# Two recurrent heads in one group of small matmuls, pairs of column sums, and an edited order, in a hybrid decoder layer

## The chip, the cores and the metric

The kernel runs on one core of a Trainium2 chip. The metric is the device time of one execution in microseconds (us); a result is the median of several executions. TensorE (PE in the profile) multiplies matrices, VectorE (DVE) and ScalarE (ACT) work elementwise, GpSimd (POOL) does some fills and scalings and issues DMAs, SyncE (SP) issues DMAs. Matrix results land in PSUM, everything else lies in SBUF. PEld is TensorE's loading of the stationary operand, which the profile shows as an engine of its own.

## What is computed

One decoder layer for 512 positions of width 1024, in float32. The normed input goes through one projection into three head groups, and their outputs through one output projection; a gated feed-forward layer follows. Cut to the parts that the change touches:

```python
h = rmsnorm(x, norm_mix)
proj = h @ w_in
y_mla = mla_group(...)      # 4 heads, low-rank q and kv, per-head norm of q and k, causal softmax
y_hg = hgrn2_group(...)     # 4 heads of a gated recurrence, width 128
y_mem = mem_group(...)      # 4 heads, normed q and k, 256 fixed memory tokens
x = x + concat(rmsnorm(y_mla), y_hg, rmsnorm(y_mem)) @ w_out
h2 = rmsnorm(x, norm_ffn)
x = x + (silu(h2 @ w_gate) * (h2 @ w_up)) @ w_down

# the recurrence of one head, by position:  f = lb + (1 - lb) * sigmoid(f_raw);  k = 1 - f
# state = f[:, None] * state + k[:, None] * v[None, :];  o = q @ state
# then a norm of o over the head's 128 columns, and a SiLU gate
```

## The kernel before

The 512 positions are columns (S = 512, four blocks of 128, NB = 4), features are partitions (P = 128). Every large product is three matmuls of split operands: a float32 is split into a high part in the faster format (`split`, line 485: a copy or scaled copy on ScalarE) and a low part (a subtraction on DVE), and `mm3` (line 515) multiplies high by high, high by low and low by high. `piece` (line 500) does that for 512 columns of a weight that `load` (line 493) has brought into a `wr` buffer through SyncE's queue; hence the tiles `wh` and `wl`.

**The order of the work** is not that of the code. `Recorder` (line 46) records every operation with its operands and a priority: the class (0, 1 or 2, set by `rec.first`) times a million, plus the number of the operation. `run` (line 241) then plays the list through with a cost for each operation (`price`, line 184) and latencies between the engines, and picks for every engine, whenever it comes free, the ready operation of lowest priority; some operations it may give to another engine. Buffers belong to tags (`BUFS`, line 426: so many of each), and an operation that opens a new buffer waits until one of its tag is free. `issue` (line 362) writes out what comes out of it, so that each engine's instructions stand in that order; they run in it, one after the other, each waiting for its operands. All instructions carry line 382 or, for groups of small matmuls, line 379: the tile names tell them apart.

**Start (lines 465 to 618).** Eight gains come first, through ScalarE's queue (line 466). Seven warm-up matmuls of 128 columns run on TensorE (line 476). The input x comes in eight tiles `tm` through SyncE's queue; each is split into `xh` and `xl`, with the gain as scale. The weights of two first projections (`EARLY`, line 396) come in five pieces into `p` and `tc` buffers, two through ScalarE's queue and three through SyncE's between the x tiles. The squares of x are summed into `td`; `colsum` (line 534), `rms` and `spread` make the row of inverse norms `RX`, by which every projection is scaled.

**Groups of small matmuls.** An operation called `tiles` is a list of matmuls on 32 columns of the stationary operand, each at its own place of the array's columns; the planner prices it at 180 ns and 64 for each part that falls on one place. One part is two instructions in the trace. `colsum` sums over the partitions of a square: 16 parts for four blocks, with `ones` as the moving operand, on a `tr` or `mm` bank. It is called for RX, for each head's norm in the recurrence, for the memory tokens, for the two low-rank norms, for each of the four query heads of the latent attention (line 928) and of the memory attention (line 1123), and for group norms.

**The recurrence (lines 744 to 820).** For one head, `hg_levels` computes the 512 x 512 matrix of decayed scores in levels m = 1, 2, 4, ... 128: between two neighbouring runs of m positions the scores are products of q and k, scaled by decays towards the border between them. Up to level 16 this is `scores`: a group of 16 parts, 32 x 32 blocks on the diagonal; of its result DVE keeps by a mask (`copy_predicated` into `cc`) what belongs to the level, and the group for the diagonal itself comes first of all. Level 32 is a group of 8 parts, level 64 four matmuls, level 128 two. After each level q, k and the decays `tot` are multiplied up in place by three DVE operations; so a group must have read them before, and the next group needs the result. Scores lie in `p` (two buffers: one for the scores, one for the decays), `at` banks hold the results of the groups. `hg_out` splits the scores, multiplies them with the values, and norms. Lines 847 to 851 go through the heads one after the other, the projections of heads 2 and 3 between them. `hg_final` (line 822) applies the gate much later and splits the output into `xh` and `xl`, which the projections of x hold until then.

**Around it.** The memory tokens are loaded into `td` (line 859) and split into `mx`; `lowrank` (line 876) projects for the latent attention and puts its squares into `td`, which has three buffers. The norm over the latent attention's heads (`group_norm`, line 1040, called in line 1131) splits into `mx`. The output projection starts with the recurrent heads (`OUT_ORDER`), then the latent heads; the memory heads are added in a second pass. The feed-forward layer takes the second half of the time.

Of the kernel before, what the change touches and what calls it, by code (L numbers as in the profile page):

```python
# [45 lines left out]
class Recorder:  # L46
# [137 lines left out]
    def price(self, o, outs, ins):  # L184
# [55 lines left out]

    def run(self):
        ops = self.ops
        for o in ops:
# [151 lines left out]
WARM = 7  # L395
EARLY = {0: (1, "p", "scalar"), 1: (2, "p", "scalar"), 3: (2, "tc", "sync"), 5: (2, "tc", "sync"), 7: (1, "tc", "sync")}
# [10 lines left out]
def body(ctx, tc, t):  # L407
# [14 lines left out]
    def nm(p):  # L422
# [5 lines left out]
        "pth": 2, "ptl": 2, "qr": 1, "p": 2, "mx": 8, "cc": 2, "sm": 12, "sd": 8, "mm": 3, "at": 3, "tr": 2,  # L428
# [27 lines left out]


# [7 lines left out]
    with rec.first(0):  # L465
        A.dma_start(out=sm[:, 0:8], in_=t["sm"][:, 0:8])
# [67 lines left out]
    def colsum(sq, nblk):  # L534

        o = ps_ts()
        T.tiles(o[:, 0:2 * nblk], lhsT=sq, rhs=ones, parts=[
            (o[g:g + 32, 2 * b:2 * b + 2], sq[:, b * P + g:b * P + g + 32], ones, b == 0, b == nblk - 1)
            for b in range(nblk) for g in range(0, P, 32)
        ])  # L540
        return o[:, 0:2 * nblk].rearrange("p (b two) -> p b two", two=2)[:, :, 0]
# [26 lines left out]
    def heads(ap):  # L568
        return ap.rearrange("p (h d) -> p h d", d=P)


    with rec.first(0):
# [3 lines left out]
        early = ([], [])  # L576
        for k in range(KD):
            if k in EARLY:
                n, tag, q = EARLY[k]
                w = sb(tag)[:, :2 * n * P]  # L580
                getattr(rec, q).dma_start(out=w, in_=t["we"][:, 2 * k * P:2 * (k + n) * P])
                pc = piece(w, 0, 2 * n * P)
# [6 lines left out]
            split(r, hi, lo, smc("g_mix", k))  # L589
# [154 lines left out]
    def hg_levels(q, k_, tot):  # L744
        A_ = sb("p", (P, NB, P))
        tt = sb("p")
        C = sb("cc", (P, NB, 32))
        toff = 0

        def scores():  # L750

            o = ps_at()[:, 0:NB * 32].rearrange("p (b t) -> p b t", t=32)
            T.tiles(o, lhsT=k_, rhs=q, parts=[
                (o[g:g + 32, b], k_[:, b * P + g:b * P + g + 32], q[:, b * P + g:b * P + g + 32], b == 0, b == NB - 1)
                for b in range(NB) for g in range(0, P, 32)
            ])
            return o

        o = scores()
        V.tensor_tensor(C, o, eye.unsqueeze(1).broadcast_to([P, NB, 32]), ALU.mult)  # L760
        G.memset(A_, 0.0)
        V.tensor_tensor(q, q, tot, ALU.mult)
        m = 1
        while m <= 128:
            if m <= 16:
                o = scores()
                V.copy_predicated(C, lmask[:, LEVELS.index(m), :].unsqueeze(1).broadcast_to([P, NB, 32]), o)
                if m == 16:
                    for g in range(0, P, 32):
                        A.copy(A_[g:g + 32, :, g:g + 32], C[g:g + 32])  # L770
            elif m == 32:
                o = heads(ps_at())[:, :, :32]
                T.tiles(o, lhsT=k_, rhs=q, parts=[
                    (o[i:i + 32, b], k_[:, b * P + i:b * P + i + 32], q[:, b * P + i + 32:b * P + i + 64], b == 0, b == NB - 1)
                    for b in range(NB) for i in (0, 64)
                ])
                for i in (0, 64):
                    A.copy(A_[i:i + 32, :, i + 32:i + 64], o[i:i + 32])
            elif m == 64:
                o = heads(ps_at())[:64, :, :64]  # L780
                for b in range(NB):
                    T.matmul(o[:, b], lhsT=k_[:, b * P:b * P + 64], rhs=q[:, b * P + 64:(b + 1) * P], start=b == 0, stop=b == NB - 1, skip_group_check=True)
                A.copy(A_[:64, :, 64:], o)
            else:
                pts = [new_pt(2), new_pt(4)]
                for g, pt in enumerate(pts):
                    for x in pt:
                        G.memset(f(x)[:, 4 * g + 2, :], 0.0)
                o = ps_at()
                for i, s in enumerate((0, 2)):  # L790
                    T.matmul(o[:, i * P:(i + 1) * P], lhsT=k_[:, s * P:(s + 1) * P], rhs=q[:, (s + 1) * P:(s + 2) * P], start=i == 0, stop=i == 1, skip_group_check=True)
                for i in range(2):
                    split(o[:, i * P:(i + 1) * P], pts[i][0][:, 4 * i + 1, :], pts[i][1][:, 4 * i + 1, :])
            n = S // (2 * m)
# [662 lines left out]
```

## Time and profile before

| | |
|---|---|
| median of 3 runs | 729.4 us (727.81 to 729.68) |
| the profiled execution | 726.6 us |
| its span, first to last instruction | 724.7 us |
| mean granted TensorE clock | 0.995 |
| DMA traffic | 98.07 MB, 135 GB/s |
| LDWEIGHTS and matmuls on 32 columns in the recurrence | 832 each, 34.6 to 133.5 us |

A line of operations gives engine, operation, output<-inputs by tag (buffer numbers left out) and shape, then the count, busy time and mean duration, and the idle time of the engine ahead of them with what ended it. In the timeline the first two columns are start and duration in us, and square brackets hold the idle time ahead and its releaser. Matmuls are pipelined: one starts before the one ahead has ended, so their busy times overlap, and starts tell more than durations.

### The profile page before, as it was taken

What the parts mean: (1) busy time and instruction counts of PE and PEld (TensorE: products, weight loads), DVE (VectorE), ACT (ScalarE), POOL (GpSimd) and SP (SyncE); (2) the same over time, 40 slices, a digit from 0 to 9 for tenths busy, and PEclk for the clock granted to TensorE, in tenths of its full rate; (3) what the DMA queues carried; (4) which work ended last, traced back from release to release, by engine and by line L of the source; (5) the groups of instructions that cost most, each with busy time, mean ns of one, the idle gap of its engine ahead of it and who ended that gap; (6) DMA issues with size and microseconds to landing.
All of it is one profiled execution on the core that took longest, in us unless ns stands there. A gap on an engine that the chain in (4) does not pass through costs nothing.

```text
span 724.7 us, 13261 instructions
## 1 busy us (share of the span) xinstructions
PE 704.3 (97%) x4808; PEld 584.5 (81%) x4808; DVE 563.0 (78%) x1326; ACT 382.6 (53%) x726; POOL 93.0 (13%) x129
## 2 busy tenths in 40 slices
PE   7999999799999999899999999999999999999997
PEld 6888777678788887688686888888888899999886
DVE  6888889869988799897899979947548677538742
ACT  6743443437684487556477674635543355543420
POOL 0000000000000000000223323213202303410000
PEclk9999999999999999999999999999999999999999
DMA  8232122014621142121999999968958757942241
GB/s 277 76 107 70 60 89 74 24 38 140 195 97 34 55 137 92 49 59 44 263 266 214 256 215 226 229 151 220 219 146 165 180 135 172 219 110 41 66 131 72
DMA packets 47873, 98.07 MB, mean 135 GB/s; under 512 B 5568, under 2 KB 15680, under 8 KB 47808
## 3 DMA queue, kind: packets, MB, share of 16 engines
q1 hardware_dynamic: 33552, 73.75, 31.3%
q0 software_dynamic: 13824, 23.07, 20.3%
q8 instruction: 38, 0.62, 0.3%
q10 hardware_dynamic: 432, 0.40, 0.2%
q14 instruction: 27, 0.22, 0.1%
HBM read 95.11 MB, written 2.10 MB: 134 GB/s over the span
## 4 chain that ended last, share of the span: by engine, by line
PE 90%; DVE 6%; ACT 2%; issue 1%; DMA 0%; DVEq 0%; ACTq 0%
PE mm L382 47%; PE tr L382 21%; PE at L382 20%; PE at L379 1%; DVE wl L382 1%; PE tr L379 1%; DVE ptl L382 1%; DVE hd L382 1%; ACT L382 1%; DVE y L382 1%; DVE sm L382 0%; ACT p L382 0%; DMA tm<-in_xT 0%; DVE tm L382 0%; DVE tc L382 0%
## 5 line engine op out<-in xcount | busy, mean ns | idle before, releaser
L382 ACT CAST wh<-wr 128x512 fp32r<-128x512 f32 (+2 forms) x136 | 80.8, 598 | 113.7 <-PE mm L382 64.9
L382 DVE TENSOR_TENSOR wl<-wr,wh 128x512 fp32r<-128x512 f32 (+2 forms) x148 | 96.5, 657 | 33.2 <-issue 11.4
L382 PE MATMUL mm<-xh,wh 128*128 128x512 f32 x248 | 99.4, 406 | 5.5 <-ACT wh L382 3.2
L382 PE MATMUL mm<-xh,wl 128*128 128x512 f32 x248 | 100.2, 405 | 0.0
L382 PE MATMUL mm<-xl,wh 128*128 128x512 f32 x248 | 99.9, 404 | 0.2 <-DVE xl L382 0.2
L382 DVE TENSOR_TENSOR wl<-y,wh 128x512 fp32r<-128x512 f32 (+1 forms) x84 | 53.1, 637 | 42.2 <-PE tr L382 17.3
L382 ACT CAST wh<-y 128x512 fp32r<-128x512 f32 (+1 forms) x83 | 48.2, 582 | 66.5 <-PE at L382 34.2
L382 DVE TENSOR_TENSOR wl<-mx,wh 128x512 fp32r<-128x512 f32 (+1 forms) x72 | 45.6, 642 | 27.6 <-PE tr L382 14.8
L382 PE MATMUL mm<-wh,hd 128*128 128x512 f32 (+2 forms) x188 | 64.0, 366 | 0.7 <-ACT wh L382 0.7
L382 ACT CAST wh<-mx 128x512 fp32r<-128x512 f32 (+1 forms) x65 | 37.8, 584 | 40.9 <-PE at L382 22.1
L382 PEld LDWEIGHTS mm<-xh,wh 128*128 128x128 f32 x248 | 47.1, 191 | 14.5 <-ACT wh L382 3.6
L382 PEld LDWEIGHTS mm<-xl,wh 128*128 128x128 f32 x248 | 47.5, 191 | 8.7 <-DVE xl L382 0.7
L382 PEld LDWEIGHTS mm<-xh,wl 128*128 128x128 f32 x248 | 47.2, 190 | 8.4
L382 PE MATMUL at<-wh,hd 128*128 128x512 f32 (+1 forms) x132 | 49.7, 377 | 0.0
L382 POOL DMA_DIRECT2D y<-in_wu x36 | 32.5, 943 | 96.9 <-DVE wl L382 80.7
L382 PE MATMUL tr<-xl,wh 128*128 128x512 f32 x112 | 43.8, 391 | 0.0
L382 PE MATMUL tr<-xh,wl 128*128 128x512 f32 x112 | 43.7, 390 | 0.0
L382 PE MATMUL tr<-xh,wh 128*128 128x512 f32 x112 | 43.7, 390 | 0.0
L382 PEld LDWEIGHTS mm<-wh,hd 128*128 128x128 f32 x188 | 34.6, 188 | 5.8 <-ACT wh L382 1.1
L382 PE MATMUL mm<-wl,hd 128*128 128x512 f32 (+2 forms) x100 | 37.0, 370 | 0.2 <-DVE wl L382 0.2
L382 POOL MEMSET p<- 128x128 f32 (+1 forms) x12 | 3.7, 312 | 258.1 <-PE tr L382 116.8
L382 PE MATMUL mm<-wh,v 128*128 128x512 f32 (+1 forms) x96 | 36.1, 376 | 0.6 <-ACT v L382 0.6
(371 smaller groups left out, 1750.5 us busy)
## 6 DMA issues: line engine op xcount, KB each, us to landing
wr<-in_wf SPq DMA_DIRECT2D x19, 512.0 KB, 3.4
wr<-in_wd SPq DMA_DIRECT2D x16, 512.0 KB, 5.2
mx<-in_wg SPq DMA_DIRECT2D x24, 256.0 KB, 5.6
mx<-in_wu SPq DMA_DIRECT2D x24, 256.0 KB, 4.8
y<-in_wu POOLq DMA_DIRECT2D x24, 256.0 KB, 6.0
tm<-in_xT SPq DMA_DIRECT2D x16, 256.0 KB, 3.6
wr<-in_wt SPq DMA_DIRECT2D x8, 512.0 KB, 4.1
wr<-in_wo SPq DMA_DIRECT2D x8, 512.0 KB, 3.5
```

The costliest lines, as they stand in the source:

```text
L379: r = self.nc.tensor.matmul(get(a), lhsT=get(b), rhs=get(c), start=first, stop=last, skip_group_check=True)
L382: r = getattr(getattr(self.nc, o.eng), o.name)(*[get(a) for a in o.args], **{k: get(a) for k, a in o.kw.items()})
```

## The change

In words. (1) `hg_levels` takes two heads: scores, masks and buffers of both stand side by side in one group and one DVE call, and the diagonal shares the group of level 1 by writing q times its decay to a new `y` buffer. Level 64 becomes a group too. The decays are multiplied up in place, and both `p` buffers hold scores. Level 128 moves to `hg_out`. (2) `colsums` sums several squares in one group; the query heads of both attentions use it in twos. (3) All five pieces of first weights go through ScalarE's queue, the eight gains lie in the first of them, `hpi` is made on ScalarE by a multiplication instead of a fill on DVE, and the warm-up is twelve matmuls of 512 columns. (4) Memory tokens are loaded into `y` instead of `td`, the gated recurrent outputs go to `mx` instead of `xh` and `xl`, the latent attention's to `xh` and `xl` instead of `mx`. (5) The planner prices a group at 310 ns and 1.81 for each column streamed at one place (at least 35 for a part). (6) `NUDGE` adds a number to the priorities of 17 stretches of operations.

```diff
-                return 180 + 64 * len(o.kw["parts"]) / len({self._rng(p[0])[2] for p in o.kw["parts"]})
+                return 310 + 1.81 * sum(max(35, self._free(p[2])) for p in o.kw["parts"]) / len({self._rng(p[0])[2] for p in o.kw["parts"]})
...
+    NUDGE = ((2868, 2885, -117), (1571, 1576, -1459), (2382, 2422, -477), (1732, 1734, 30), (826, 835, 186), (957, 1012, 3), (5620, 5660, 284), (3804, 3864, -113), (987, 1017, 110), (2666, 2693, -105), (2466, 2475, -61), (2533, 2540, 37), (2401, 2403, -37), (3367, 3411, -5), (3019, 3021, 346), (16, 18, 380), (2, 19, 3),)
...
+        for a, b, d in self.NUDGE:
+            for o in ops[a:b]:
+                o.prio += d
...
-WARM = 7
-EARLY = {0: (1, "p", "scalar"), 1: (2, "p", "scalar"), 3: (2, "tc", "sync"), 5: (2, "tc", "sync"), 7: (1, "tc", "sync")}
+WARM = 12
+EARLY = {0: (1, "p"), 1: (2, "p"), 3: (2, "tc"), 5: (2, "tc"), 7: (1, "tc")}
...
-    with rec.first(0):
-        A.dma_start(out=sm[:, 0:8], in_=t["sm"][:, 0:8])
...
-            T.matmul(o[:, 0:P], lhsT=ones_r, rhs=ones_r, start=True, stop=True)
+            T.matmul(heads(o), lhsT=ones_r, rhs=ones_r.unsqueeze(1).broadcast_to([P, NB, P]), start=True, stop=True)
     hpi = cp.tile([P, 1], F32, name="hpi")
-    V.memset(hpi, float(np.pi / 2))
...
+    def colsums(sqs, nblk=NB):
+        o = ps_ts()[:, 0:2 * nblk * len(sqs)]
+        ks = [(i, b) for i in range(len(sqs)) for b in range(nblk)]
+        v = o.rearrange("p (i b two) -> p i b two", two=2, b=nblk)
+        T.tiles(o, ones, *sqs, parts=[
+            (v[g:g + 32, i, b], sqs[i][:, b * P + g:b * P + g + 32], ones, (i, b) == ks[0], (i, b) == ks[-1])
+            for i, b in ks for g in range(0, P, 32)
         ])
-        return o[:, 0:2 * nblk].rearrange("p (b two) -> p b two", two=2)[:, :, 0]
+        return v[..., 0]
...
+        for k, (n, tag) in EARLY.items():
+            w = ws[k] = sb(tag)[:, :2 * n * P + 8 * (k == 0)]
+            A.dma_start(out=w, in_=t["we"][:, 2 * k * P + 8 * (k > 0):2 * (k + n) * P + 8])
+        gain = ws[0][:, 2 * P:]
+
+        A.mul(hpi, ones[:, 0:1], float(np.pi / 2))
...
+    def hg_levels(hs):
+
+        N2 = range(len(hs))
+        As = [sb("p", (P, NB, P)) for i in N2]
+        C = sb("cc", (P, len(hs), NB, 32))
+        old, hs = hs, [(sb("y"), k_, tot) for q, k_, tot in hs]
+
+        def scores(sets):
+
+            n = len(sets) * len(hs)
+            o = ps_at()[:, 0:n * NB * 32].rearrange("p (n b t) -> p n b t", t=32, b=NB)
+            ps_ = [(b, g) for b in range(NB) for g in range(0, P, 32)]
+            all_ = [(i * len(hs) + j, h) for j in N2 for i, s in enumerate(sets) for h in (s[j],)]
+            T.tiles(o, *[x for i, h in all_ for x in h[:2]], parts=[
+                (o[g:g + 32, i, b], h[1][:, b * P + g:b * P + g + 32], h[0][:, b * P + g:b * P + g + 32], (i, b) == (all_[0][0], 0), (i, b) == (all_[-1][0], NB - 1))
+                for i, h in all_ for b, g in ps_
             ])
+            return [o[:, i * len(hs):(i + 1) * len(hs)] for i in range(len(sets))]
...
+        for (q, _, tot), (q1, _, _) in zip(old, hs):
+            V.tensor_tensor(q1, q, tot, ALU.mult)
...
+            if m == 1:
+                o, o1 = scores([old, hs])
+                V.tensor_tensor(C, o, eye.unsqueeze(1).unsqueeze(1).broadcast_to([P, len(hs), NB, 32]), ALU.mult)
+                put(o1, 1)
+            elif m <= 16:
+                put(scores([hs])[0], m)
...
+            hs = [(q, k_, step_up(q, k_, tot, m)) for q, k_, tot in hs]
...
-        hi = sb("xh", dt=F32R)
-        lo = sb("xl", dt=F32R)
+        hi = sb("mx", dt=F32R)
+        lo = sb("mx", dt=F32R)
         split(y, hi, lo)
         mix[4 + h] = (hi, lo)
...
-    for h in (0, 1):
-        yh.append(hg_out(h, *hg_levels(*qkf[h])))
-    qkf += [hg_in(2), hg_in(3)]
-    for h in (2, 3):
-        yh.append(hg_out(h, *hg_levels(*qkf[h])))
+    for h, st in enumerate(hg_levels(qkf)):
+        yh.append(hg_out(h, *st))
+    qkf = [hg_in(2), hg_in(3)]
+    for h, st in enumerate(hg_levels(qkf)):
+        yh.append(hg_out(2 + h, *st))
...
-            r = sb("td", (P, 2, NM))
+            r = sb("y", (P, 2, NM))
...
-            sq = sumsq([o])
-            V.tensor_copy(vq[:, :, h], colsum(sq, NB))
+            sq.append(sumsq([o]))
+            if h % 2:
+                V.tensor_copy(vq[:, :, h - 1:h + 1].rearrange("p b h -> p h b"), colsums(sq[-2:]))
...
-    group_norm(ym, 0, "g_mla", ("mx", "mx"))
+    group_norm(ym, 0, "g_mla", ("xh", "xl"))
```

More of the change, by code (lines that the diff above doesn't have):

```diff
@@ L455, in small, with heads @@
         return sb("sm" if rec.cls == 1 else "sd", (P, 16))[:, :n]
+    def heads(ap):
+        return ap.rearrange("p (h d) -> p h d", d=P)
     cst = cp.tile([P, 2 * P + 64], F32, name="cst")
@@ L534, in colsum @@
     def colsum(sq, nblk):
[L536 to L539, printed above, removed]
+        return colsums([sq], nblk)[:, 0]
+    def colsums(sqs, nblk=NB):
[5 more added lines that the diff above has]
+            for i, b in ks for g in range(0, P, 32)
         ])
-        return o[:, 0:2 * nblk].rearrange("p (b two) -> p b two", two=2)[:, :, 0]
+        return v[..., 0]
     def spread(r):
@@ L588, in body @@
             lo = sb("xl", dt=F32R)
-            split(r, hi, lo, smc("g_mix", k))
+            split(r, hi, lo, gain[:, k:k + 1])
             xg.append((hi, lo))
@@ L768, in hg_levels @@
                 if m == 16:
-                    for g in range(0, P, 32):
-                        A.copy(A_[g:g + 32, :, g:g + 32], C[g:g + 32])
+                    for j in N2:
+                        for g in range(0, P, 32):
+                            A.copy(As[j][g:g + 32, :, g:g + 32], C[g:g + 32, j])
             elif m == 32:
[L772 to L775, printed above, removed]
-                ])
@@ L777, in hg_levels @@
[L777 to L783, printed above, removed]
-            else:
[L785 to L793, printed above, removed]
@@ new lines, in hg_out @@
+    def hg_out(h, A_, q, k_, tot):
+        pts = [new_pt(2), new_pt(4)]
+        for g, pt in enumerate(pts):
+            for x in pt:
+                G.memset(f(x)[:, 4 * g + 2, :], 0.0)
+        o = ps_at()
+        for i, s in enumerate((0, 2)):
+            T.matmul(o[:, i * P:(i + 1) * P], lhsT=k_[:, s * P:(s + 1) * P], rhs=q[:, (s + 1) * P:(s + 2) * P], start=i == 0, stop=i == 1, skip_group_check=True)
+        for i in range(2):
+            split(o[:, i * P:(i + 1) * P], pts[i][0][:, 4 * i + 1, :], pts[i][1][:, 4 * i + 1, :])
+        step_up(q, k_, tot, 128)
```

83 lines of the change are left out of this document (41 added, 42 removed).

## The prediction

> **What bounds the kernel now.** I read the page first, then the windows by stage, then the timeline around single operations.
>
> ```profile
> span 724.7 us, 13261 instructions
> ...
> PE 704.3 (97%) x4808; PEld 584.5 (81%) x4808; DVE 563.0 (78%) x1326; ACT 382.6 (53%) x726; POOL 93.0 (13%) x129
> ...
> PE 90%; DVE 6%; ACT 2%; issue 1%; DMA 0%; DVEq 0%; ACTq 0%
> ```
>
> TensorE is busy for 704.3 of 724.7 us and carries 90% of the chain that ends last. So an edit is worth what it takes off TensorE's queue, plus what it takes out of the 20.4 us in which TensorE is idle. The windows say where that idle time lies (columns: window, its length, then busy us of PE, PEld, DVE, ACT, POOL; granted clock; DMA).
>
> ```profile
> 72.50:90.60 18.10, 18.10 (x196) 14.10 (x195) 15.87 (x43) 7.81 (x15) 0.91 (x3) 1.00 0.20 60
> ...
> 126.80:145.00 18.20, 14.26 (x174) 11.05 (x173) 15.49 (x49) 8.63 (x20) 0.20 (x1) 0.91 0.08 23
> ...
> 290.00:308.00 18.00, 14.44 (x95) 11.09 (x94) 15.20 (x40) 9.20 (x20) 0.96 (x2) 0.91 0.13 47
> ...
> 453.00:600.00 147.00, 146.84 (x692) 123.04 (x691) 97.82 (x158) 72.78 (x127) 34.60 (x40) 1.00 0.78 179
> ```
>
> The feed-forward half (the last row is 147 us of it) leaves nothing idle: what the change moves there can only lose. Two stages leave much: 3.94 us where the last recurrent head overlaps the memory loads (stall one), 3.56 us around the attention norm (stall two). In both the granted clock falls to 0.91. If it is halved for x us, the mean over 18 us falls by 9% when x is 3.3, and that costs up to 1.6 us more of TensorE time. So the stalls are worth up to 5.5 and 5.2 us.
>
> **The groups of small pieces.** What is one group worth? Two column sums stand close together, one of 32 instructions, one of 16; below them stands a score group, with 32 columns instead of two.
>
> ```profile
> 147.04 0.39 PE L382 MATMUL mm<-xh,wh 128*128 128x512 f32 x1
> 147.36 0.43 PE L379 MATMUL tr<-ones,tc 128*32 128x2 f32 x32
> 147.72 0.50 PE L382 MATMUL mm<-xl,wh 128*128 128x512 f32 x1
> 148.06 0.40 PE L382 MATMUL mm<-xh,wl 128*128 128x512 f32 x1
> 148.39 0.31 PE L379 MATMUL tr<-ones,td 128*32 128x2 f32 x16
> 148.62 0.50 PE L382 MATMUL mm<-xh,wh 128*128 128x512 f32 x1
> 148.96 0.39 PE L382 MATMUL mm<-xl,wh 128*128 128x512 f32 x1
> ```
>
> ```profile
> 70.28 0.39 PE L382 MATMUL mm<-xl,wh 128*128 128x512 f32 x1
> 70.50 0.40 PE L382 MATMUL mm<-xh,wl 128*128 128x512 f32 x1
> 70.83 0.46 PE L379 MATMUL at<-tm,tm 128*32 128x32 f32 x32
> 71.22 0.50 PE L382 MATMUL mm<-xh,wh 128*128 128x512 f32 x1
> 71.56 0.39 PE L382 MATMUL mm<-xl,wh 128*128 128x512 f32 x1
> ```
>
> Busy times overlap here, so I count from start to start. With no group between them, one matmul starts 0.22 us after the other (70.28 to 70.50); I use 0.23. From 147.04 to 148.06 lie two such steps and the group of 32: 1.02 - 0.46 = 0.56 us. From 148.06 to 148.96 lie two steps and the group of 16: 0.90 - 0.46 = 0.44. Sixteen instructions more cost 0.12, so 32 cost 0.24, and the rest, 0.32, is paid once for a group whatever is in it. The score group: 70.50 to 71.56 is 1.06 - 0.46 = 0.60; less 0.24, 0.36 is paid once.
>
> ```profile
> L379 PE MATMUL at<-tm,tm x832: 189/196/247, 34.6 to 133.5; 128*32 128x32 f32 x167
> ```
>
> 832 instructions are 24 groups of 32 and 4 of 16 (level 32). For a pair of heads the code goes from 12 groups of 32 to one of 128 and four of 64: 7 fixed parts fewer. Level 32 goes from two groups to one, and level 64, written as single matmuls until now, from two sets to one; I price that set at the same 0.36 by its likeness, an estimate between nothing and twice that. Nine times 0.36 is 3.24 a pair, 6.5 us for both. The number of instructions is the same. The four query heads of the latent attention and of the memory attention now share a column sum in twos: 4 groups fewer, 4 x 0.32 = 1.3. Together **7.8 us**, all on TensorE's queue; bounds 5.2 (two thirds, if a large group hides its drain less well) and 9.
>
> [...]
>
> What hides the rest of this edit is DVE, which has slack (78%): it writes each first q product to a new buffer instead of in place, which is the same operation, and masks two heads in one call. The wait that the edit adds: one group now waits for the updates of both heads, with TensorE's matmuls queued in order behind it.
>
> ```profile
> L382 DVE TENSOR_TENSOR tm<-tm,p 128x256 f32<-128x256 f32 x56 | 22.4, 417 | 0.0
> ```
>
> That is 4 x 0.417 = 1.67 us of updates ahead of a group instead of 0.83. In return there are 14 such rounds instead of 28. In the row 72.50:90.60 the projections between the groups keep TensorE busy for all 18.10 us, so I price the wait at nothing, and put its loss into a rival.
>
> **The start.**
>
> ```profile
> 1.22 1.76 PE L382 MATMUL tr<-ones_r 128*128 128x128 f32 x7 [1.22 <-DVE ones_r L382]
> ...
> 3.78 1.28 ACT L382 ACT_TABLE_LOAD   x1 [3.78 <-DMA tm<-in_xT]
> ...
> 5.07 0.72 ACT L382 ACTIVATE xh<-tm,smv 128x512 fp32r<-128x512 f32 x1
> ...
> 6.14 1.22 PE L382 MATMUL mm<-xh,wh 128*128 128x512 f32 x2 [3.17 <-ACT wh L382]
> ...
> 9.29 0.63 PE L382 MATMUL mm<-xl,wh 128*128 128x512 f32 x1
> ...
> 26.00 0.59 ACT L382 COPY RX<-tr 128x512 f32<-128x512 f32 x1 [0.43 <-PE tr L382]
> ```
>
> ScalarE's first table load waits for the first x to land and only then takes 1.28 us. The new multiplication for hpi needs only ones, so the load runs ahead of the data. ScalarE's queue also gets five weight DMAs in place of three DMAs: two more issues, and each is still ahead of the data; SyncE has three fewer ahead of x. So the first split can start up to 1.28 us earlier, less what x loses to five weight loads that now run beside it. Twelve warm-up matmuls of 512 columns, in place of seven of 128, start at 1.22 and take 0.23 us each at the full clock and twice that at half, so they end between 4.0 and 6.7. If the clock comes up in them, real matmuls find it up; before, it was still half at 9.29 (0.63 us against the 0.40 above). That could give some 2 us more, but the first projections must be scaled by RX, copied at 26.00 behind eight splits, squares and sums, and TensorE would come early to a wait. I take **1.0 us**, between 0 and 2.5. Merging the eight gains into the first weights takes one small DMA out.
>
> **The stalls and the order.** Two rows of stall one:
>
> ```profile
> 130.40 0.46 PE L379 MATMUL at<-tm,tm 128*32 128x32 f32 x32 [2.41 <-DVE tm L382]
> ...
> 131.94 0.50 PE L382 MATMUL mm<-xh,wh 128*128 128x512 f32 x1 [1.08 <-ACT td L382]
> ```
>
> The second is a matmul that waits for a bank whose square needs one of the three td buffers, while the memory loads hold td. The change puts those loads into y, so this 1.08 should go, and some of the 2.41 with DVE's shorter list: **1.5 us**, between 0 and 5.5. In stall two the norm's split now goes to xh and xl, and the recurrent outputs to mx, which they need not wait for xh to come free: **0.7**, between 0 and 5.2.
>
> The 17 stretches are positions in the list of recorded operations (the new list is 46 shorter). At the start two weight loads go behind a third on ScalarE's queue. In the second pair of heads the steps of levels 4 and 8 go 186 later, and the last head's rescaling with the first memory loads (SyncE DMAs, their splits on ScalarE and DVE) 110 later, behind those levels and behind the last memory load on SyncE's queue. One head's q split in the latent attention goes to the front of its class. The first memory head's scores, softmax (with GpSimd's scaling) and products go 477 earlier, ahead of the norm of stall two; three small stretches of the same attention go by 37 to 61, and four others by 3 to 30. In the output projection two stretches with their SyncE loads go 105 and 117 earlier, one matmul and its low part 346 later. The feed-forward's second gate loads (SyncE, and GpSimd's adding DMAs) go 113 earlier, past the splits ahead of them; the last weight splits go 284 later. None removes an instruction. With TensorE busy throughout the feed-forward half, I take nothing for those, and for the others nothing beyond the 1.5 and 0.7; the bound on both sides is the two stalls, 10.7 us. The new price of a group (563 ns for 32 where the list was planned with 436, beside the 600 measured) makes the planned order fit the chip better, which speaks for the gain's side.
>
> Sum: 7.8 + 1.0 + 1.5 + 0.7 = 11.0. The profiled execution took 726.6 (span 724.7 and 1.9 around it), 2.8 below the median of the runs, 729.4; 715.6 on its scale is **718.4** on the median's.
>
> **The rivals.** *Only the groups count.* The stalls stay or move elsewhere, and at the start the weights take from x what the table load gives: all of it shares the same transfers. 729.4 - 7.8 = 721.6. For it: the 1.0, 1.5 and 0.7 are small parts of waits with several causes. [...]
>
> *The order is right as well.* Both stalls go, and the start gives its 2.5: 7.8 + 2.5 + 10.7 = 21.0, so 708.4. Against it: the norm in stall two is a serial chain with three banks ahead of it.
>
> *The price goes by instruction.* Nothing is saved by merging and the small terms drown: 729.4. [...]
>
> *The pair starves TensorE.* A group must wait for four updates, and if there are no projections to put between, 0.83 us more are bare at each of the 14 rounds: 11.7 us. With the groups' 7.8 and the start's 1.0 against it, 729.4 + 11.7 - 8.8 = 732.3. It decides from (8.8 + 2.2) / 14 = 0.79 us bare a round. Stall one is just this kind of wait (2.41 <-DVE tm), in the last of the four heads, where little was left to put in; against it stands that 14 rounds need less filling than 28.
>
> **How the numbers follow.** Forecast 0.55 (its own range 714 to 722), only the groups 0.20, order right too 0.12, price by instruction 0.07, starved 0.06. The runs lie within 0.26% of each other, so 0.3%, 2.2 us, is about what can be told. Faster is the sum of the first three, 0.87; the same 0.07; slower 0.06. 711 to 725 takes in the first two and half of the third, and leaves out 0.19.
>
> **What would show it.** The group rows should read x128 and x64, at 0.36 + 0.24 for each 32 from start to start (0.84 for 64, 1.32 for 128); TensorE's instructions differ only by the five warm-up ones. The table load should stand ahead of 3.78, and the first real matmul by 6 with the clock up. RX should be copied near 25.0. No ACT td wait in the memory stage; granted clock 1.00 in stall one. Wrong would be: groups of 64 at 1.2 us, more idle time with DVE tm as the releaser in the recurrence, a feed-forward half longer than before, or a wait of the same size that has only moved.

## The result and the profile after

The changed kernel takes **707.88 us** (median of four executions, 707.76 to 707.98) against 729.08 of the kernel before beside it (727.81 to 729.68): 0.971 times, 95% interval 0.9695 to 0.9728. It is 21.2 us faster where 11.0 were forecast, and below the range.

From the page after: the span, the engines, and the chain that ended last.

```profile
span 706.0 us, 13190 instructions
...
PE 697.1 (99%) x4813; PEld 581.1 (82%) x4813; DVE 552.4 (78%) x1295; ACT 384.8 (55%) x740; POOL 93.4 (13%) x128
...
PE 91%; DVE 5%; DMA 1%; ACT 1%; issue 1%; SPq 0%; DVEq 0%; ACTq 0%
```

The span is 18.7 us shorter. (The profiled execution before, 726.6, lay 2.5 below the median of its runs; that is the rest of the 21.2. It goes with the clock: over the span this execution was granted 0.995, other executions of the kernel before 0.990 to 0.991 at about 728.4 us and 0.988 at about 729.4, and those of the changed kernel 0.997 to 1.000.) TensorE's idle time falls from 20.4 to 8.9 us, its busy time by 7.2, although the warm-up alone is 3.7 longer. The windows after, with the columns and the stretches of before:

```profile
72.50:90.60 18.10, 18.10 (x161) 14.84 (x160) 15.68 (x52) 11.76 (x24) 2.05 (x7) 1.00 0.26 88
126.80:145.00 18.20, 17.89 (x168) 14.64 (x167) 15.97 (x65) 8.41 (x23) 0.71 (x4) 1.00 0.09 30
290.00:308.00 18.00, 18.00 (x105) 15.26 (x103) 16.24 (x44) 12.57 (x33) 0.00 (x0) 1.00 0.25 74
344.00:362.00 18.00, 17.46 (x77) 13.42 (x76) 17.97 (x37) 13.32 (x26) 1.29 (x2) 1.00 0.99 270
453.00:600.00 147.00, 147.00 (x698) 125.59 (x698) 96.45 (x159) 71.92 (x126) 36.24 (x42) 1.00 0.76 171
```

Of the kernel before, the fourth stretch and one further on:

```profile
344.00:362.00 18.00, 16.50 (x103) 12.53 (x103) 15.87 (x35) 8.66 (x15) 3.63 (x4) 1.00 0.94 257
380.00:398.00 18.00, 16.72 (x70) 12.47 (x70) 17.80 (x40) 12.54 (x24) 7.02 (x9) 1.00 0.94 211
```

Both stalls are gone, with the low clock that came with them: 3.94 us of idle time in the second row have become 0.31, 3.56 in the third have become nothing, and the clock is 1.00 where it was 0.91. The feed-forward half is as full as before. What TensorE still waits for (us in total, times, longest):

```profile
PE mm L388 <- ACT xh L388: 1.2, 1, 1.2
PE tr L388 <- DVE ones_r L388: 1.2, 1, 1.2
PE mm L388 <- DVE wl L388: 0.4, 1, 0.4
```

The first two are the start. Behind it no wait reaches half a microsecond. Now a group of 64 pieces, with its neighbours:

```profile
108.71 0.39 PE L388 MATMUL mm<-xl,wh 128*128 128x512 f32 x1
109.03 0.76 PE L385 MATMUL at<-y,tm 128*32 128x32 f32 x64
109.72 0.51 PE L388 MATMUL mm<-xh,wl 128*128 128x512 f32 x1
110.06 0.39 PE L388 MATMUL mm<-xh,wh 128*128 128x512 f32 x1
```

From 108.71 to 110.06 lie 1.35 us, less two steps of 0.23: 0.89 for the group, where 0.84 were forecast. Read in the same way over both traces, a group of 128 takes 1.43 (forecast 1.32), and two groups of 32, at 0.59 each, are what one of 64 replaces. Last, the start:

```profile
1.22 5.49 PE L388 MATMUL tr<-ones_r 128*128 128x512 f32 x12 [1.22 <-DVE ones_r L388]
1.66 1.28 ACT L388 ACT_TABLE_LOAD   x1 [1.66 <-PEq L1482]
...
4.32 2.49 ACTq L388 DMA_DIRECT2D tc<-in_we  x2
6.85 0.40 ACT L388 CAST wh<-p 128x256 fp32r<-128x256 f32 x1 [3.69 <-DMA p<-in_we]
7.16 0.72 ACT L388 ACTIVATE xh<-tm,p 128x512 fp32r<-128x512 f32 x1
...
7.93 0.73 PE L388 MATMUL mm<-xh,wh 128*128 128x512 f32 x2 [1.22 <-ACT xh L388]
```

```profile
26.40 0.59 ACT L388 COPY RX<-tr 128x512 f32<-128x512 f32 x1 [2.54 <-PE tr L388]
```

The table load is early (1.66, where it stood at 3.78) and the clock is up, as forecast: from 9.05 on matmuls start 0.23 to 0.24 us apart, where they started 0.43 apart before (8.87, 9.29, 9.72). But the first split of x comes at 7.16, not ahead of 5.07, and RX is copied 0.40 later than before: ScalarE stood behind its own last two weight DMAs, whose issue took 2.49 us, up to 6.81. (The row at 6.85 names the DMA of the first weights as what it waited for; a version below uses the same weights at 4.42.)

An account from these rows: groups 6.2 (worked out below), stall one 3.63 of idle time and 1.6 of clock (the prediction's upper estimate), stall two 3.56 and 1.6, two later waits (344 to 362: 1.50 to 0.54 idle; 380 to 398: 1.28 to 0.06) 2.2, less 0.4 at the start: 18.4 of the 18.7. So the stalls and the later waits gave 12.6 where the forecast had 2.2. Most of that, 10.4, is the two stalls that the prediction had named and counted in small part. What removed them?

### The profile page after: what moved, and what is told of

The parts are those of the page before. It is cut to its first block, busy times and chain, and to the rows that moved or that the text cites. A ratio compares the mean times of both kernels' runs of the same rounds, so it can differ in the third digit from the quotient of the medians.

```text
span 706.0 us, 13190 instructions
## 1 busy us (share of the span) xinstructions
PE 697.1 (99%) x4813; PEld 581.1 (82%) x4813; DVE 552.4 (78%) x1295; ACT 384.8 (55%) x740; POOL 93.4 (13%) x128
## 3 DMA queue, kind: packets, MB, share of 16 engines
q0 software_dynamic: 13824, 23.07, 20.5%
## 4 chain that ended last, share of the span: by engine, by line
PE 91%; DVE 5%; DMA 1%; ACT 1%; issue 1%; SPq 0%; DVEq 0%; ACTq 0%
PE mm L388 46%; PE at L388 21%; PE tr L388 21%; PE at L385 1%; DVE wl L388 1%; DVE y L388 1%; DMA tm<-in_xT 1%; DVE tm L388 1%; DVE td L388 1%; PE tr L385 1%; DMA wr<-in_wf 1%; DVE xl L388 0%; DVE hd L388 0%; DVE v L388 0%; ACT wh L388 0%
## 5 line engine op out<-in xcount | busy, mean ns | idle before, releaser
L388 ACT CAST wh<-y 128x512 fp32r<-128x512 f32 (+1 forms) x81 | 46.7, 580 | 67.5 <-PE at L388 36.7
L388 PEld LDWEIGHTS mm<-xl,wh 128*128 128x128 f32 x248 | 46.6, 188 | 10.4 <-DVE xl L388 2.2
L388 PE MATMUL at<-wh,v 128*128 128x512 f32 (+1 forms) x96 | 35.8, 375 | 0.0
```

The source lines that it names most:

```text
L388: r = getattr(getattr(self.nc, o.eng), o.name)(*[get(a) for a in o.args], **{k: get(a) for k, a in o.kw.items()})
```

## The experiments

**Theory A, the order:** the new price and the 17 stretches fill the stalls. **Theory B, the buffers:** memory loads in `y` and the exchanged halves take away waits for space. The forecast's own view, a rival of both, is that each stall has several causes and the edit meets only a part.

### Taking parts out of the changed kernel

**No stretches.**

```diff
-    NUDGE = ((2868, 2885, -117), ... (2, 19, 3),)
+    NUDGE = ()
```

> The changed kernel with an empty list of stretches; price, buffers, pairs and start as changed. The traces of before and after show 7.3 us less lost in 275 to 300, 4.7 less in 125 to 150 and 3.1 less in 350 to 400. Theory A, the order: the stretches are what emptied these places, so most of it comes back, 715 to 720. Theory B, the buffers: the two stalls ended because tiles no longer wait for each other's space, and the stretches only trim, so only the 3.1 of 350 to 400, where no buffer changed, comes back: 711.

Measured: 712.16 us (0.9771 of before, 0.9756 to 0.9785). The stretches are worth 4.3, less than A, more than B. The waits that return:

```profile
283.15 0.74 PE L388 MATMUL mm<-xh,wh 128*128 128x512 f32 x2 [1.25 <-ACT xh L388]
```

```profile
337.54 0.73 PE L388 MATMUL mm<-xh,wh 128*128 128x512 f32 x2 [2.26 <-ACT xh L388]
```

Stall one stays away, and half of stall two.

**No stretches, old price.**

```diff
-return 310 + 1.81 * sum(max(35, self._free(p[2])) for p in o.kw["parts"]) / ...
+return 180 + 64 * len(o.kw["parts"]) / ...
```

> As the kernel without stretches, and a group is planned again at 180 + 64 for each four pieces. Theory A: the price decides where groups stand, so planning 32-piece groups too cheaply opens waits again: 3 to 5 us above the kernel without stretches. Theory B: within 1 us of it, since a planner that errs by 0.13 us a group on 14 groups errs by 2 us in all and has matmuls to fill in.

Measured: 719.21 (0.987, 0.9855 to 0.9884). 7.0 above the kernel without stretches: more than A asked for. The largest single wait is at 343.48, 3.40 for a norm's small statistics (DVE sm), some 200 us behind the last group of scores; around it only a few column sums have this price. The stage 272 to 290 loses too: its idle time grows from 1.83 to 3.65 us, and its clock falls from 1.00 to 0.83.

**Old buffers.**

```diff
-            r = sb("y", (P, 2, NM))
+            r = sb("td", (P, 2, NM))
...
-        hi = sb("mx", dt=F32R)
-        lo = sb("mx", dt=F32R)
+        hi = sb("xh", dt=F32R)
+        lo = sb("xl", dt=F32R)
...
-    group_norm(ym, 0, "g_mla", ("xh", "xl"))
+    group_norm(ym, 0, "g_mla", ("mx", "mx"))
```

> The changed kernel with the four loads of the memory back in td, the attention norm's halves back in mx and the recurrent outputs' halves back in xh and xl; stretches, price, pairs and start as changed. Theory A: 708 to 710. Theory B: both stalls return, 12.0 us by the two traces less what the groups save there (about 1): 717 to 720.

Measured: 724.79 (0.995, 0.9935 to 0.9964). 16.9 of the 21.2 are lost: theory B, and by more than the two stalls.

**Old start.**

```diff
-WARM = 12
-EARLY = {0: (1, "p"), 1: (2, "p"), 3: (2, "tc"), 5: (2, "tc"), 7: (1, "tc")}
+WARM = 7
+EARLY = {0: (1, "p", "scalar"), 1: (2, "p", "scalar"), 3: (2, "tc", "sync"), 5: (2, "tc", "sync"), 7: (1, "tc", "sync")}
...
+    V.memset(hpi, float(np.pi / 2))
...
-        A.mul(hpi, ones[:, 0:1], float(np.pi / 2))
```

> The changed kernel with the start as it was: seven warm-up matmuls of 128 columns, the gains loaded by themselves, three of the five first weight loads on SyncE's queue, hpi by VectorE; the two stretches at the start are left out with it, the others stay on the same operations. By the prediction's term: 708.9, 1.0 slower. By the traces (the first column sum stands at 22.04 where it stood at 21.46): within 0.7 of 707.9, to either side.

Measured: 707.13 (0.9706, 0.969 to 0.9722), RX copied at 25.83. The new start brings nothing; by the medians it loses 0.75. The forecast's term is out; the reading by the traces had allowed 0.7 to either side.

### Single parts on the kernel before

If buffers are worth 16.9, they should show alone.

**Groups alone** (pairs of heads and of column sums; price, buffers, start as before).

> The kernel before with the pairs of heads and the pairs of column sums alone; price, buffers, start as before, no stretches. The groups of the changed kernel, read from start to start, take 1.43 (128 pieces), 0.89 (64) and 0.98 (32 of level 32) where the kernel before pays 0.59 for 32 and 0.63 for 16: worked out, 6.2 us less. If they are worth that by themselves: 722 to 724. If the pair's longer chain of updates eats it, with the old plan and buffers: 728 or more, with TensorE waiting for DVE tm in the second pair.

Measured: 725.10 (0.9955, 0.994 to 0.997): 3.3, of 6.2. Most of the rest goes into stall one, which has grown:

```profile
120.59 0.45 PE L385 MATMUL at<-y,tm 128*32 128x32 f32 x16 [3.38 <-DVE tm L388]
...
123.57 1.94 PE L385 MATMUL at<-y,tm 128*64 128x64 f32 x16 [1.87 <-DVE tm L388]
126.33 0.79 PE L388 MATMUL mm<-xh,wh 128*128 128x512 f32 x1 [0.81 <-ACT td L388]
```

6.1 us of waits where before had 2.41, 1.08 and 0.45, 2.1 more.

**Buffers alone** (the old-buffers diff, reversed, on the kernel before).

> The kernel before with the three changes of buffers alone (memory loads in y, attention norm's halves in xh and xl, recurrent outputs' halves in mx), planned anew. Theory B, the buffers by themselves hold the gain beyond the groups: both stalls go, 5.5 + 5.2, 718 to 720. Rival: the old price still places groups too early, so that other waits take their place: 724 to 729.

Measured: 729.45 (1.0011, 1.0002 to 1.002). Nothing is gained. Stall one is gone (window 126.8 to 145: 17.77 of 18.20 busy, clock 1.00), but there are new waits at 28.20 (0.82), 29.50 (0.68) and 52.94 (0.82), and the 1.25 that stood at 352.12 has become 3.48 for DVE sm at 353.74. Stall two has not gone: in 290 to 308 TensorE is idle for 2.03 us at a clock of 0.81. The rival's reading, waits in new places, holds; its number, 724 to 729, just misses.

**Price alone.**

> The kernel before with the new price of a group alone, planned anew. If the price is worth what it was in the changed kernel (719.2 against 712.2): 722. If it only pays once the buffers let the planner choose: 727 to 730.

Measured: 726.97 (0.9987, 0.9972 to 1.0003): perhaps 1.5, perhaps nothing; it was not the 7 that it was in the changed kernel.

**Weights on SyncE.** The last three loads of first weights go back to SyncE's queue, in their old places between the loads of x, and the two stretches at the start are left out; the rest of the new start stays.

```diff
-            A.dma_start(out=w, in_=t["we"]...)
+            (A if k < 3 else DMA).dma_start(out=w, in_=t["we"]...)
```

> The changed kernel with the last three of the five first weight loads on SyncE's queue again, each in its old place between the loads of x, and without the two stretches of the start; early table load, twelve warm-up matmuls and merged gains stay. The old start as a whole was 0.75 faster than the new one. Theory: ScalarE's queue was held by the fourth load (2.49 us at 4.32) and the splits behind it came late, so 706.3 to 707.0. Rival: the longer warm-up is what costs, so no change, 707.9.

Measured: **706.15** (0.9694, 0.9678 to 0.971), the fastest version. Its start:

```profile
4.42 0.41 ACT L388 CAST wh<-p 128x256 fp32r<-128x256 f32 x1 [1.26 <-DMA p<-in_we]
4.74 0.72 ACT L388 ACTIVATE xh<-tm,p 128x512 fp32r<-128x512 f32 x1
...
5.78 0.62 PE L388 MATMUL mm<-xh,wh 128*128 128x512 f32 x2
```

```profile
24.66 0.58 ACT L388 COPY RX<-tr 128x512 f32<-128x512 f32 x1 [0.21 <-PE tr L388]
```

The split of x starts at 4.74, the first real matmul at 5.78, and RX is copied 1.74 earlier than in the changed kernel. So early table load, long warm-up and merged gains bring 1.2 at RX (25.83 in the old start, 24.66 here), close to the forecast's 1.0, and the three DMAs on ScalarE's queue cost 1.7, there and in the whole time, and turn it into a loss.

### Which buffer, and is the price a truth or a draw

**Memory loads in td** (the first hunk of the old-buffers diff alone).

> The changed kernel with the four memory loads alone back in td; everything else as changed. All three buffers back cost 16.9 us, with a wait of 3.64 (DVE tm) and one of 1.32 (ACT td) at the last two heads. If those two waits and the half clock behind them belong to the loads: about 7 us, 714 to 716. If the loads only matter beside the halves: under 2, 708 to 710.

Measured: 723.58 (0.9927, 0.99 to 0.9954): 15.7 lost, twice the expected 7. Both waits of stall one are back,

```profile
122.52 1.30 PE L385 MATMUL at<-y,tm 128*32 128x32 f32 x32 [3.64 <-DVE tm L388]
125.15 0.80 PE L388 MATMUL mm<-xh,wh 128*128 128x512 f32 x1 [1.32 <-ACT td L388]
```

and so is stall two (0.75, 1.48, 0.56 and 0.62 between 281 and 292), to which these loads have no direct tie: what is planned behind them changes as well.

**Halves as before** (the two other hunks alone).

> The changed kernel with the attention norm's halves back in mx and the recurrent outputs' halves back in xh and xl; the memory loads stay in y. If the waits at 280 to 293 of the kernel with all three back (0.96 xh, 1.61 tc, 0.56 and 0.63 hd, and the clock at 0.83) belong to these tiles: about 9 us, 715 to 718, and the last two heads stay free of waits. If the planner would have found another filling: under 3.

Measured: 713.17 (0.9792, 0.977 to 0.9813). 5.3 lost, between the two expectations; the last two heads stay free of waits, and there are three waits behind (1.04 at 283.19, 1.02 at 339.74, 0.71 at 370.10).

**Price 5 per cent up, and down** (without stretches: 330 + 1.9 and 290 + 1.72).

> The changed kernel without stretches, a group planned at 330 + 1.9 for each column in place of 310 + 1.81 (595 ns for 32 pieces in place of 563, 862 for 64 in place of 817; measured are 590 and 890). The old price, 436 and 692, gave 719.2, the new one 712.2. Theory T, the truth pays: nearer to the measured cost is as good or better, 711 to 713. Theory L, each price is another draw of the order: anywhere between 710 and 720, 715 or more as likely as not.

> As the one before, with 290 + 1.72: 531 ns for 32 pieces, 772 for 64. Theory T: a quarter of the way back to the old price costs at most a quarter of 7 us: 712 to 714. Theory L: anywhere between 710 and 720.

Measured: 715.67 (0.9824, 0.9805 to 0.9843) and 719.21 (0.9866, 0.9845 to 0.9886). Theory L holds. 596 ns for 32 pieces is nearer to the measured 590 than 563 is, and 3.5 slower; 531 already gives the time of the old price, 436. Its wait stands at the same place as the old price's:

```profile
344.02 0.77 PE L388 MATMUL tr<-td,ones_r 128*128 128x512 f32 x1 [3.58 <-DVE sm L388]
```

Four prices between 436 and 596 give 719.2, 719.2, 712.2, 715.7. Each redraws the order, and the new price was a good draw. So the 7.0 do not measure what the old price was wrong by.

### With the order held

What are the buffers worth when the order cannot answer?

**Order of before, new buffers.** The planned order of the kernel before was written into the kernel, instruction by instruction and engine by engine, and the tags alone changed.

```diff
-    order = rec.run()
+    order = rec.held_order()
```

> The kernel before with its planned order written down and held, instruction by instruction, and the three new buffers alone. Theory: the order was planned around the old buffers, so nothing in it can start much earlier; the one wait for a td bank (1.08 at 131.94) goes and the 2.41 behind DVE stays: 726 to 729, within 2 of before. Rival: the two stalls are waits for space, and they go in any order: 718 to 722.

Measured: 728.51 (1.0002, 0.9992 to 1.0011). Nothing, as the theory had it. First the row of before that follows the two quoted in the prediction, then the same place here:

```profile
133.12 0.58 PE L379 MATMUL at<-tm,tm 128*32 128x32 f32 x15 [0.45 <-DVE tm L382]
```

```profile
130.36 0.46 PE L392 MATMUL at<-tm,tm 128*32 128x32 f32 x32 [2.41 <-DVE tm L395]
...
133.08 0.64 PE L392 MATMUL at<-tm,tm 128*32 128x32 f32 x16 [1.60 <-DVE tm L395]
```

The 1.08 for a td bank is gone, and the next wait has grown from 0.45 to 1.60, by 1.15. In this fixed order the removed wait only moved to the next producer in line. Stall two stays as well: 3.09 us idle in 290 to 308, at a clock of 0.72.

**No stretches, old buffers.**

> The changed kernel without stretches and with the three old buffers: pairs, new price and new start. Beside it stands the same with new buffers, 712.2. If the 16.9 of the old buffers was the buffers' own: 725 to 729. If a good part was that the stretches did not fit the old buffers: 718 to 722.

Measured: 726.65 (0.9975, 0.9964 to 0.9987): 14.5 above the same with new buffers. So at most 2.4 of the 16.9 came from stretches that no longer fitted. The windows, with old buffers and then with new:

```profile
108.70:126.80 18.10, 12.93 (x261) 9.92 (x261) 17.92 (x52) 8.04 (x17) 0.00 (x0) 0.89 0.23 75
...
290.00:308.00 18.00, 16.26 (x67) 13.18 (x67) 14.76 (x41) 9.39 (x22) 0.48 (x1) 0.72 0.09 31
```

```profile
108.70:126.80 18.10, 17.81 (x313) 13.62 (x301) 17.03 (x57) 7.82 (x16) 0.00 (x0) 1.00 0.15 47
...
290.00:308.00 18.00, 18.00 (x105) 15.37 (x104) 16.69 (x42) 12.78 (x32) 0.48 (x1) 1.00 0.27 84
```

DVE is as busy in both first rows (17.92 and 17.03): it is TensorE that finds nothing to do beside it, 5.2 us idle with the old buffers.

**Memory stretches alone.** Of the 17, the four in the memory attention.

```diff
+    NUDGE = ((2382, 2422, -477), (2466, 2475, -61), (2533, 2540, 37), (2401, 2403, -37))
```

> The changed kernel with the four stretches in the memory attention alone (first head 477 earlier, three others). The traces without stretches lose 2.1 more in 275 to 300 and 3.5 more in 325 to 350 than with all. If these four hold the gain: 707 to 709. If it takes the others too, since each moves what stands behind it: 711 to 716.

Measured: 715.21 (0.9821, 0.9798 to 0.9844): 3 us *slower* than with none. Two windows without stretches, and the same with these four:

```profile
326.00:344.00 18.00, 15.49 (x96) 11.56 (x95) 14.02 (x31) 7.60 (x13) 6.44 (x7) 0.91 0.87 265
434.00:453.00 19.00, 18.84 (x98) 15.22 (x98) 18.73 (x31) 11.71 (x21) 7.01 (x8) 1.00 1.09 262
```

```profile
326.00:344.00 18.00, 18.00 (x114) 14.40 (x113) 15.41 (x34) 8.24 (x14) 5.19 (x6) 1.00 0.75 243
434.00:453.00 19.00, 16.47 (x79) 12.68 (x78) 17.95 (x30) 8.41 (x16) 6.10 (x7) 0.91 0.98 219
```

They empty the first window of its wait and open one of 2.14 (DVE ptl) in the second, 100 us later. So these four do not hold the 4.3, and what a stretch does depends on the others. Which of the rest hold it is not shown.

**Groups twice.** In the changed kernel's own order, each group of scores is issued twice in a row, the second overwriting the first.

```diff
-                for a, b, c, first, last in o.kw["parts"]:
+                for a, b, c, first, last in o.kw["parts"] * (2 if self._free(o.kw["parts"][0][2]) >= 32 else 1):
```

> The changed kernel in its own order, each of the fourteen groups of scores issued twice in a row, the second time overwriting the first. From start to start a further 32 pieces cost 0.27 to 0.30 here, so 8 x 0.6 + 2 x 1.1 for the score groups and some 2.6 for the levels 32 and 64: 9.6 more on TensorE. If TensorE's time counts in full in a held order: 716 to 718. If half of it falls into waits: 712 to 714.

Measured: 725.76 (0.9963, 0.995 to 0.9975): 17.9, not 9.6. TensorE's time counts in full. It is busy for 708.9 us in place of 697.1, 11.8 more, and the rest are gaps in long runs of small pieces:

```profile
61.04 0.83 PE L385 MATMUL at<-y,tm 128*32 128x32 f32 x73
62.73 0.46 PE L385 MATMUL at<-y,tm 128*32 128x32 f32 x32 [0.86 <-issue]
```

```profile
43.65 0.22 PE L385 MATMUL at<-tm,tm 128*32 128x32 f32 x2 [2.37 <-issue]
```

Five such gaps add up to 6.1 us; more on them below.

**Buffers and price, no pairs.**

> The kernel before with the new buffers and the new price, without pairs, start or stretches. Pairs, buffers, price and start together took 712.2. If the pairs are worth their 6.2 and no more, this stands 6.2 above that, 718 to 720, and the wait at the last two heads (126 to 133) is gone. If the new buffers only pay with the shorter chain of pairs: 725 to 729, with waits of the norm (DVE sm) in place of the old ones.

Measured: 725.66 (0.9958, 0.9942 to 0.9975), 13.5 above the kernel without stretches, of which the groups explain 6.2 (the start, which is also the old one here, would take off 0.75). The waits of before are smaller (0.69 at 130.36, 1.61 at 293.19, 1.25 at 349.05) and new ones stand at 28 to 53, as with the buffers alone. Of the rest, some 7 to 8 us, I have no closer account.

**The changed kernel again.**

> The changed kernel as it is. If the difference of 1.7 to the version with three weights on SyncE (706.15, 0.9694 of before) is of the kernels: 707.5 to 708.3, 0.970 to 0.972 of before. If it is of the chips: 706 to 707.

Measured: 708.31 (0.9719, 0.9705 to 0.9734). So the lead of the version with three weights on SyncE, 1.7 to 2.2 us, is of the kernels and not of the chips; RX is copied here at 26.53, again some 1.9 later than there.

### What the runs settle

| kernel | pairs | buffers | price | start | stretches | us |
|---|---|---|---|---|---|---|
| before | | | | | | 728.4 to 729.1 |
| buffers only | | new | | | | 729.5 |
| price only | | | new | | | 727.0 |
| buffers and price | | new | new | | | 725.7 |
| groups only | new | | | | | 725.1 |
| no stretches, old buffers | new | | new | new | | 726.7 |
| no stretches, old price | new | new | | new | | 719.2 |
| no stretches | new | new | new | new | | 712.2 |
| changed | new | new | new | new | new | 707.9 |

Shown: of the parts tried alone, none is worth more than 3.3 us (the new start was not tried alone), and the last two rows lose 14.5 and 16.9 us if the buffers go. The buffers act through the order: in the order of before they are worth nothing. And stall one hangs on one tag. Every kernel that was planned with the memory loads in td waits 2.4 to 3.6 us for DVE tm at the last heads (six kernels); of those planned with the loads in `y`, none waits more than 0.7 there. Theory B is right about the cause and wrong about the way, theory A about the way and wrong about the price. Which TensorE work the td buffers kept from standing ahead of those groups, the traces show. It is the low-rank products of the latent attention: each fills one of three `mm` banks, and the bank comes free only when its square has been written to a td buffer. Here is such a square in the changed kernel, then the first of them with the memory loads in td:

```profile
111.83 0.59 ACT L388 ACTIVATE td<-mm 128x512 f32<-128x512 f32 x1
```

```profile
124.50 0.60 ACT L388 ACTIVATE td<-mm 128x512 f32<-128x512 f32 x1 [0.25 <-DVE mx L388]
```

In the changed kernel three of these five squares (105.37, 111.83, 118.16) are done among the last heads' groups. In the six kernels planned with the loads in td the first comes at 124 to 131, once TensorE already stands in the wait or behind it; in all those planned with the loads in `y`, at 103 to 119. Not shown is why stall two answers to so many edits; that a fuller choice lets the planner find better draws there is argued only.

## Why the prediction was wrong, point by point

**The groups: mechanism right, 7.8 forecast, 6.2 worked out from the traces**, inside its bounds. (Tried alone they brought 3.3 of it.) A fixed part is paid once for a group (0.59 for 32 pieces, 0.89 for 64: 0.30 a further 32, so 0.29 fixed). Forecast were 0.24 and 0.36, because the 0.24 came from column sums with two columns. A pair took 12 x 0.59 + 2 x 0.63 + 2 x 0.81 = 9.96 and takes 1.43 + 4 x 0.89 + 0.98 + 1.44 = 7.41; twice 2.55 and four column sums at 0.28 are 6.2. Level 64 saves 0.18 a pair, not the 0.36 taken by likeness. (Two of these figures are rough: the groups of level 64 take 1.59 in the first pair and 1.28 in the second, and the 0.98 of level 32 is the second pair's, with 0.81 in the first; read pair by pair the sum is 6.4.)

**The start: wrong sign.** The step that failed is "two more issues, and each is still ahead of the data". Two of ScalarE's issues took 2.49 us at 4.32 and stood ahead of its first split. The other half of that part was right: without these DMAs on ScalarE's queue, RX is copied at 24.66, near the 25.0 forecast, and the first real matmul starts at 5.78. The first loads of x landed later beside the weights, as a rival had it: the first two took 3.0 and 3.5 us from issue to landing before and 3.4 and 5.0 after (all eight, in the median, 5.9 and 5.4), with the DMA engines full in both starts (share 1.04 and 0.99 from 3 to 6 us) and both queues on them (76.6 and 11.8 per cent of the first 14 us before, 68.4 and 20.5 after). The first split, at 7.16, came some 3 us behind the first of these landings.

**The stalls: the step that failed.** "This 1.08 should go, and some of the 2.41 with DVE's shorter list: 1.5 us", 0.7 for stall two, and "for the others nothing beyond". In the order of before the 1.08 did go and came back as 1.15 at the next wait: by the prediction's own way of working, removing a wait from a given order, the term would have been nothing. But the order is planned anew, and there the loads' tag decided over the 2.41 as well, which the prediction had put down to DVE. The row names the producer that came last; it does not say why TensorE had nothing else in line. The reason, products waiting for td, stood one row below it. Both stalls went in full: up to 5.2 each instead of 1.5 and 0.7, and 2.2 more in 344 to 398, where nothing was forecast.

**The bound was right, its chance was not.** The rival "the order is right as well" gave 708.4. Its total came out by terms that cancel: groups 1.6 less, start 2.5 plus 0.4 less, against the waits at 344 to 398 and the profile's 2.5. It was priced at 0.12, since "the norm in stall two is a serial chain with three banks ahead of it". Ten other orders with pairs do show waits between 273 and 296; those of the changed kernel and of its two versions with another start do not. The prediction had no means of telling this order from those.

**The starved pair** was right in one setting: with pairs and the old buffers stall one grows from 3.9 to 6.1 us. **Price by instruction** is out: two groups of 32 take 1.18, one of 64 takes 0.89. **Feed-forward nothing** holds: 147.00 of 147.00.

## What to carry to other kernels

Where a planner writes the order, an edit of buffers or prices is an edit of the whole order: bound it by the idle time and the lowered clock (0.91 in both stalls here) in the stages that it touches, both ways, and take each stall as kept or gone rather than in fractions. Read a stall by the second row too: the wait for space next to a long wait for data may be the cause of both. Before giving credit to a tuned constant, move it by 5 per cent; here that moved the time by 3.5 and 7 us, as much as the groups were worth.

## What the runs showed of the hardware

**Long runs of small matmuls showed gaps without a producer.** The page's instruction queue, after and with groups twice:

```profile
q8 instruction: 37, 0.61, 0.3%
```

```profile
q8 instruction: 44, 0.72, 0.4%
```

864 more matmuls and as many weight loads came with 7 more packets; by these figures a packet holds about 250 instructions, an estimate. A run of 128 pieces is 256 instructions and takes 1.43 us; the changed kernel's two such groups pass without a gap, but in the doubled groups gaps of 2.37, 0.86 and 1.91 us "<-issue" appear (and two of 0.5), and in the second pair 256 pieces took 4.61 us where 2.6 were worked out (1.43 + 4 x 0.30). What causes the gaps is not shown by any run here. A group of four heads would be such a run of 256 pieces all the same.

**A wait of 1.61 us, with one of 0.41 behind it, cost the clock.** From the kernel with buffers and price:

```profile
293.19 0.50 PE L382 MATMUL mm<-xh,wh 128*128 128x512 f32 x1 [1.61 <-DVE xh L382]
293.52 0.51 PE L382 MATMUL at<-hd,hd 128*128 128x256 f32 x3
294.45 0.80 PE L382 MATMUL mm<-xl,wh 128*128 128x512 f32 x1 [0.41 <-DVE xl L382]
295.04 0.63 PE L382 MATMUL mm<-xh,wl 128*128 128x512 f32 x1
295.47 0.63 PE L382 MATMUL mm<-xh,wh 128*128 128x512 f32 x1
```

Behind the two waits the matmuls start 0.43 apart instead of 0.23, for six steps, until 4.4 us after the first wait; the six cost 1.2 us, and the granted clock is 0.91 over 290 to 308. In the kernel without stretches a single 1.25 at 283.15 had no such effect: the two matmuls there take 0.74 together, and the clock is 1.00 over 272 to 290. So in this one place 2.0 us of waits cost 3.2 in all.

**DMA issues on ScalarE's queue were ScalarE's time.** Two issues took 2.49 us there while SyncE's eight took 7.01 beside them, and ScalarE's next operation starts 0.04 us behind them, at 6.85; with these loads on SyncE it starts at 4.42. Here the issue time moved into ScalarE's own stream, where it cost 1.7 us (RX copied at 26.40 instead of 24.66, 707.88 us instead of 706.15).
